# Two operand buffers lent to the first HGRN2 group, eviction priority, and a new order in cross-attention: a two-layer decoder trunk on one core

## The chip, the core and the metric

The kernel runs on one NeuronCore of a Trainium2 chip. Its engines are TensorE (PE; its weight loads are listed as PEld), VectorE (DVE), ScalarE (ACT), GpSimd (POOL) and SyncE (SP), which issues most DMAs. Each engine works through its own queue in order and waits at semaphores for the others. The metric is the device time of one execution in microseconds; the times given are medians over runs.

## What is computed

The reference is a trunk of two layers over 256 tokens of width 2048, followed by an RMSNorm. Layer 0 mixes tokens with eight HGRN2 heads (a gated linear recurrence) and eight gated-DeltaNet heads (delta rule); layer 1 with a Mamba-2 SSD mixer. After each mixer come a cross-attention of four heads into 256 memory tokens and a SwiGLU network. Cut to what matters here:

```
def hgrn2_gdn_mixer(u, ...):
    proj = u @ w_in
    a_q, a_f, a_i, a_g, b_q, b_k, b_v, b_g, b_beta, b_a = split(proj)
    o_a = hgrn2_chunked(silu(a_q), (1 - lb) * sigmoid(-a_f), a_i, log(lb + (1 - lb) * sigmoid(a_f)))
    o_a = gated_head_norm(o_a, hgrn_norm, a_g)       # times silu(a_g)
    o_b = gated_delta_chunked(...)                   # on silu(conv(b_q, b_k, b_v))
    o_b = gated_head_norm(o_b, gdn_norm, b_g)
    return concatenate([o_a, o_b]) @ w_out

def memory_cross_attention(h, m, wq, wk, wv, wo):
    q, k, v = heads(h @ wq), heads(m @ wk), heads(m @ wv)
    p = softmax(q k^T * 128 ** -0.5)
    return (p v) @ wo
```

## The kernel before

**Matmuls in three products.** Weights and activations are float32. Both are split into a high part in TensorE's float32r format and a low rest, and a product is summed from high x high, high x low and low x high. `xstat` (L183) does a projection of all 256 tokens onto up to 512 columns: two accumulators in PSUM (two token halves, from the pool `pa`, four buffers) and, for 16 tiles of 128 rows, 2 x 3 matmuls: 96 of 128x512. `wtiles` (L160) feeds it: a DMA of 512 KB into `wr`, a cast by ScalarE into `wh` (L157), a subtraction by VectorE into `wl` (L125), with four buffers of each. One such tile holds two of the 16 row blocks and feeds 12 matmuls.

**Leaving the accumulators.** `rows` copies the two accumulators through ScalarE, scaled by the norm's factor `r`, into the tile "raw" (one buffer). Where the function is a sigmoid, VectorE multiplies once more by the scaled input, which makes SiLU. `columns` then turns "raw" by TensorE transposes into the PSUM tile `tn`. `gate_rows` does the same without turning, into a tile of its own: "gate" or "vt" in the hybrid mixer, "XT" in attention. Each of these tags has one buffer: the next user waits until the last reader of the one before is done.

**The order.** The program is traced in Python order; a planner then orders the queue of every engine by simulating a timeline with its own durations. Of the instructions that it holds ready it takes the one that stands earliest in the program, and buffers are given out as they come free in that simulation. `later` pins some DMAs in program order.

**Layer 0's mixer** (`hybrid`) traces gdn(0), gdn(1), hgrn(0), hgrn(1) and then the output projection in two halves: `project(Wo, yb, 8, 8)` for the two gdn results and `project(Wo, ya, 0, 8)` for the two hgrn results, each in four blocks of 512 columns with 48 matmuls. Each of gdn and hgrn works on four heads. gdn ends in a serial chain: its matrix goes out to DRAM and comes back re-blocked, a 16x16 inversion runs on VectorE, the results X and XT go through DRAM again, then come three doubling levels of small matmuls (L578 to L599) and the outputs. hgrn forms its scores in seven levels, each a chain over VectorE, ScalarE, GpSimd and TensorE, into the tile "D", which gdn uses for its decays `E`. `finish` multiplies by the values, `head_norm` reads the gate, `head_out` writes the two operand tiles (high and low part) into the pool "u". That pool has 16 buffers of [128, 4, 256], which also hold the eight operand tiles of the layer's normed input.

**Cross-attention** (`xattn`) projects q from the tokens and k from the memory, takes the scores for two token halves `a`, two heads at a time in a PSUM tile of the pool `pm` (three buffers), and for each half in turn: maximum, exponential with its sum, reciprocal, four multiplications, then the transposes into `pT`:

```
        for a in range(2):
            ...
            for i in range(2):
            ...
                    act.activation(pr[:, a, m], ps[:, x], AF.Exp, bias=mx[:, m:m + 1], scale=sc,
                                   accum_out=sm[:, m:m + 1])
            dve.reciprocal(sm, sm)
            for m in range(4):
                dve.tensor_scalar(pr[:, a, m], pr[:, a, m], sm[:, m:m + 1], None, op0=ALU.mult)
            for b in range(2):
            ...
                dve.tensor_copy(pT[b][:, :, a * P:(a + 1) * P], ps)
        v = gate_rows(M, ("xa_wv", layer), 0, AF.Copy, "XT")
```

After that come the value products and the output projection `xa_wo` (four row tiles, so 24 matmuls for a block).

The functions that the diff touches, and what calls them:

Of the kernel before, what the change touches and what calls it, by code (L numbers as in the profile page):

```python
# [9 lines left out]
F32 = mybir.dt.float32  # L10
# [3 lines left out]
AF = mybir.ActivationFunctionType  # L14
ALU = mybir.AluOpType
AX = mybir.AxisListType
PSUM = bass.MemoryType.PSUM

P = 128
D = 2048  # L20
T = 256
# [57 lines left out]
def trunk(ctx: ExitStack, tc: tile.TileContext, A: dict, out: bass.AP):  # L79
# [44 lines left out]
    def tt(e, o, a, b, op):  # L124
        e.tensor_tensor(o, a, b, op=op)  # L125

    def stt(o, a, s, b, op0, op1):
        dve.scalar_tensor_tensor(o, a, s, b, op0=op0, op1=op1)  # L128

    def t4(tag, shape, dt=F32):  # L130
        return mp.tile(shape, dt, name=tag, tag=tag, bufs=BUFS.get(tag, 1))
# [219 lines left out]
    def conv(c, x, w):  # L351

        act.activation(c, x, AF.Copy, scale=w[:, 3:4])  # L353
        for s in range(1, 4):
            stt(c[:, s:T], x[:, 0:T - s], w[:, 3 - s:4 - s], c[:, s:T], ALU.mult, ALU.add)

    def rows(N, W, n0, func=AF.Copy, first=None):

        accs = xstat(W, n0, 512, N.u)
        if first:  # L360
            first()
        r = N.column()
        o = t4("raw", [P, 2, 512])
        o = [o[:, 0], o[:, 1]]
        for a in range(2):
            act.activation(o[a], accs[a], func, scale=r[:, a:a + 1])  # L366
            if func == AF.Sigmoid:
                stt(o[a], accs[a], r[:, a:a + 1], o[a], ALU.mult, ALU.mult)
        return o

    def columns(N, W, n0, func=AF.Copy, first=None):
# [63 lines left out]
    def head_out(yT, norm, g):  # L435
# [5 lines left out]
            stt(lo[:, m, :], ps, w, hi[:, m, :].bitcast(F32), ALU.mult, ALU.subtract)  # L441
        return hi, lo

    def gate_rows(N, W, n0, func=AF.Silu, tag="gate", n=512):
        o = t4(tag, [P, 2, 512])
        for c in range(0, 512, n):
            accs = xstat(W, n0 + c, n, N.u)
            r = N.column()
            for a in range(2):
                act.activation(o[:, a, c:c + n], accs[a], func, scale=r[:, a:a + 1])  # L450
                if func == AF.Sigmoid:
                    stt(o[:, a, c:c + n], accs[a], r[:, a:a + 1], o[:, a, c:c + n], ALU.mult, ALU.mult)
        return o


    def hybrid(N, nxt):
        W = ("hy_w_in", 0)
# [168 lines left out]
        def hgrn(g):  # L626
            kq = t4("kq", [P, 2, 4, T])
            lf = t4("tmp", [P, 4, T])
            for i, ps in columns(N, W, 1024 + 512 * g):
                act.activation(lf[:, 2 * i:2 * i + 2], ps, AF.Sigmoid)  # L630
                act.activation(kq[:, 0, 2 * i:2 * i + 2], ps, AF.Sigmoid, scale=-1.0)
            for m in range(4):
                dve.tensor_scalar(kq[:, 0, m], kq[:, 0, m], lb[:, 1, 4 * g + m:4 * g + m + 1], None, op0=ALU.mult)
            for i, ps in columns(N, W, 512 * g, AF.Sigmoid):
                act.copy(kq[:, 1, 2 * i:2 * i + 2], ps)
            gate = gate_rows(N, W, 3072 + 512 * g, AF.Sigmoid)
            G = t4("cv", [P, 4, T])
            for m in range(4):
                l0, l1 = lb[:, 0, 4 * g + m:4 * g + m + 1], lb[:, 1, 4 * g + m:4 * g + m + 1]
                act.activation(lf[:, m], lf[:, m], AF.Ln, bias=l0, scale=l1)  # L640
                for a in range(2):
                    sl = slice(a * P, (a + 1) * P)
                    dve.tensor_tensor_scan(G[:, m, sl], lv[:, len(LEVELS), :], lf[:, m, sl], 0.0,
                                           op0=ALU.mult, op1=ALU.add)
            k, q = kq[:, 0], kq[:, 1]
            S = t4("D", [P, 12, P])
            for i in range(2):
                ps = psb([P, 4, P])
                for x in range(4):
                    m, a = i * 2 + x // 2, x % 2  # L650
                    sl = slice(a * P, (a + 1) * P)
                    mm(ps[:, x], k[:, m, sl], q[:, m, sl])
                tt(dve, S[:, 4 * i:4 * i + 4], ps, ident.unsqueeze(1).to_broadcast([P, 4, P]), ALU.mult)
            for li, s in enumerate(LEVELS):
                nb = 1024 // (2 * s)
                vw = lambda t: t.rearrange("p h (b two s) -> p (h b) two s", two=2, s=s)
                Xl = t4("tmp", [P, 4, T])
                Xv, Gv = vw(Xl), vw(G)
                ref = Gv[:, :, 0, s - 1:s].to_broadcast([P, nb, s])
                tt(dve, Xv[:, :, 0, :], ref, Gv[:, :, 0, :], ALU.subtract)  # L660
                if s < 64:
                    tt(dve, Xv[:, :, 1, :], Gv[:, :, 1, :], ref, ALU.subtract)
                    act.activation(Xl, Xl, AF.Exp)  # L663
                else:
                    act.activation(Xv[:, :, 0, :], Xv[:, :, 0, :], AF.Exp)
                    act.activation(Xv[:, :, 1, :], Gv[:, :, 1, :], AF.Exp)
                tt(pool, Xv[:, :, 0, :], Xv[:, :, 0, :], vw(k)[:, :, 0, :], ALU.mult)
                tt(pool, Xv[:, :, 1, :], Xv[:, :, 1, :], vw(q)[:, :, 1, :], ALU.mult)
                ps = psb([P, 8, 64])
                for x in range(8):  # L670
                    m, a = x // 2, x % 2
                    xa = Xl[:, m, a * P:(a + 1) * P]
                    mm(ps[:, x].rearrange("p (b s) -> p b s", s=s), xa,
                       xa.rearrange("p (b two s) -> p b two s", two=2, s=s)[:, :, 1, :])
                right = lambda t: t.rearrange("p x (b two s) -> p x b two s", two=2, s=s)[:, :, :, 1, :]
                msk = right(lv[:, li, :].unsqueeze(1))
                dve.copy_predicated(right(S[:, 0:8]), msk.to_broadcast([P, 8, 64 // s, s]).bitcast(U32),
                                    ps.rearrange("p x (b s) -> p x b s", s=s))

            Xl = t4("tmp", [P, 4, T])  # L680
            G4 = G.rearrange("p h (a two s) -> p h a two s", a=2, two=2)
            tt(dve, G4[:, :, :, 1, :], G4[:, :, :, 1, :], G4[:, :, :, 0, 63:64].to_broadcast([P, 4, 2, 64]), ALU.add)
            tt(dve, Xl[:, :, 0:P], G[:, :, P - 1:P].to_broadcast([P, 4, P]), G[:, :, 0:P], ALU.subtract)
            act.activation(Xl[:, :, 0:P], Xl[:, :, 0:P], AF.Exp)
            act.activation(Xl[:, :, P:T], G[:, :, P:T], AF.Exp)
            tt(pool, Xl[:, :, 0:P], Xl[:, :, 0:P], k[:, :, 0:P], ALU.mult)
            tt(pool, Xl[:, :, P:T], Xl[:, :, P:T], q[:, :, P:T], ALU.mult)
            ps = psb([P, 4, P])
            for m in range(4):
                mm(ps[:, m], Xl[:, m, 0:P], Xl[:, m, P:T])  # L690
            act.copy(S[:, 8:12], ps)
            v = gate_rows(N, W, 2048 + 512 * g, AF.Copy, "vt").rearrange("p a (m d) -> p a m d", m=4)
            return finish(g, v, gate, lambda m: S[:, 2 * m], lambda m: S[:, 8 + m], lambda m: S[:, 2 * m + 1],
                          "hgrn_norm", EPS)

        yb = [gdn(0), gdn(1)]


        lg = col("lb", 0, 16)
# [19 lines left out]
    def xattn(layer, N, nxt):  # L719
# [15 lines left out]
        pT = [t4(tg, [P, 4, T]) for tg in ("D", "MD")]  # L735
        pr = t4("kq", [P, 2, 4, T])
        sc = float(P) ** -0.5
        for a in range(2):
            mx = cp.tile([P, 4], F32, name="xmx", tag="xmx", bufs=1)
            sm = cp.tile([P, 4], F32, name="xsm", tag="xsm", bufs=2)  # L740
            for i in range(2):
                ps = psb([P, 2, T])
                for x in range(2):
                    m = 2 * i + x
                    mm(ps[:, x], q[:, m, a * P:(a + 1) * P], k[:, m])
                dve.tensor_reduce(mx[:, 2 * i:2 * i + 2], ps, axis=AX.X, op=ALU.max)
                dve.tensor_scalar(mx[:, 2 * i:2 * i + 2], mx[:, 2 * i:2 * i + 2], -sc, None, op0=ALU.mult)
                for x in range(2):
                    m = 2 * i + x
                    act.activation(pr[:, a, m], ps[:, x], AF.Exp, bias=mx[:, m:m + 1], scale=sc,  # L750
                                   accum_out=sm[:, m:m + 1])
            dve.reciprocal(sm, sm)
            for m in range(4):
                dve.tensor_scalar(pr[:, a, m], pr[:, a, m], sm[:, m:m + 1], None, op0=ALU.mult)
            for b in range(2):
                ps = psb([P, 4, P])
                for m in range(4):
                    pe.transpose(ps[:, m], pr[:, a, m, b * P:(b + 1) * P], ident)  # L758
                dve.tensor_copy(pT[b][:, :, a * P:(a + 1) * P], ps)
        v = gate_rows(M, ("xa_wv", layer), 0, AF.Copy, "XT")  # L760
        hi, lo = utiles()
        for i in range(2):
# [254 lines left out]
```

## Time and profile before

| | |
|---|---|
| Median of 3 runs | 3005.39 us (3005.18 to 3006.37) |
| Profiled execution | 3001.37 us, its span 2999.6 us |
| TensorE busy | 2951.6 us, 98% |
| VectorE, ScalarE, GpSimd busy | 58%, 50%, 9% |
| Mean granted clock of TensorE | 0.992 |

The profile is of one execution. Times in its rows are microseconds from the start of the span unless marked ns. A row names the line, the engine, the operation, and output<-input by the program's tile names; a count follows an x. In square brackets, or behind "idle before", stands how long the engine had waited and for what. Since a helper issues all matmuls (L122) and most VectorE operations (L125, L128), those rows are told apart by their tiles. Matmuls overlap in the pipeline, so the spacing of their starts, not their mean duration, is what one costs in a row of them.

### The profile page before, as it was taken

How to read it: one execution, taken by the hardware profiler on the slowest of the kernel's cores; microseconds unless marked ns; L12 is line 12 of the kernel's file. 1: busy time of each engine (PE TensorE's matmuls, PEld its weight loads, DVE VectorE, ACT ScalarE, POOL GpSimd, SP SyncE). 2: the span in 40 equal slices, each digit the busy share in tenths (PEclk: the TensorE clock that was granted, in tenths of full speed). 3: DMA queues.
4: the chain of work that ended last, by engine and by line, in shares of the span. 5: the costliest groups of instructions: out<-in, count | busy, mean ns of one | idle time of the engine just before them, and what ended most of it. 6: DMA issues, size and time to landing. Idle time of an engine off the chain costs nothing.

```text
span 2999.6 us, 36568 instructions
## 1 busy us (share of the span) xinstructions
PE 2951.6 (98%) x13948; PEld 2448.5 (82%) x13948; DVE 1739.2 (58%) x2154; ACT 1513.3 (50%) x1933; POOL 265.2 (9%) x209
## 2 busy tenths in 40 slices
PE   9999799999999999999999999999999999999998
PEld 7888688878888888888888788878878888888887
DVE  6665577665555445445666646666655554445455
ACT  7445364565443444344567645766555444443444
POOL 1011233020000000000022300231000000000000
PEclk9999999999999999999999999999999999999999
DMA  7555334664666666666554466455656666666664
GB/s 280 171 168 156 100 116 144 184 203 150 189 189 196 189 191 189 195 191 184 182 162 155 158 187 189 150 158 164 189 176 188 189 188 193 191 189 192 193 190 148
DMA packets 152160, 533.35 MB, mean 178 GB/s; under 512 B 16592, under 2 KB 22864, under 8 KB 151984
## 3 DMA queue, kind: packets, MB, share of 16 engines
q1 hardware_dynamic: 150096, 526.15, 56.8%
q0 software_dynamic: 1472, 4.59, 0.5%
q8 instruction: 109, 1.79, 0.3%
q14 instruction: 67, 0.55, 0.1%
q10 hardware_dynamic: 416, 0.27, 0.0%
HBM read 526.49 MB, written 4.46 MB: 177 GB/s over the span
## 4 chain that ended last, share of the span: by engine, by line
PE 93%; issue 2%; DVE 1%; DMA 1%; POOL 1%; ACT 1%; SPq 0%; DVEq 0%; ACTq 0%; POOLq 0%
PE acc L122 86%; PE mx L122 5%; PE mx L280 1%; PE tn L280 1%; POOL tmp L125 1%; DVE wl L125 0%; DMA wr<-in_memT 0%; DVE b L125 0%; PE mx L853 0%; DMA XT<-scratch 0%; DMA b<-scratch 0%; DMA scratch<-b 0%; DMA wr<-in_hy_w_in 0%; PE mx L758 0%; DVE tmp L125 0%
## 5 line engine op out<-in xcount | busy, mean ns | idle before, releaser
L122 PE MATMUL acc<-wh,u 128*128 128x512 f32 (+1 forms) x7904 | 2455.1, 390 | 6.7 <-ACT wh L157 6.7
L125 DVE TENSOR_TENSOR wl<-wr,wh 128x1024 fp32r<-128x1024 f32 x980 | 1236.2, 1265 | 1052.5 <-ACT wh L157 1049.5
L122 PEld LDWEIGHTS acc<-wh,u 128*128 128x128 f32 x7904 | 1475.4, 188 | 305.9 <-ACT wh L157 6.7
L157 ACT CAST wh<-wr 128x1024 fp32r<-128x1024 f32 x980 | 1028.6, 1052 | 1149.4 <-PE acc L122 1076.4
L122 PE MATMUL acc<-wl,u 128*128 128x512 f32 (+1 forms) x3952 | 1538.5, 389 | 3.5 <-DVE wl L125 3.4
L122 PEld LDWEIGHTS acc<-wl,u 128*128 128x128 f32 x3952 | 744.0, 188 | 153.9 <-DVE wl L125 5.0
L125 POOL TENSOR_TENSOR tmp<-gh,cst 128x512 fp32r<-128x512 f32 x36 | 49.6, 1379 | 1303.2 <-ACT gh L157 849.3
L128 DVE SCALAR_TENSOR_TENSOR cv<-tn,cols,cv 128x255 f32<-128x255 f32 (+2 forms) x120 | 57.7, 481 | 31.3 <-ACT cv L353 28.6
L125 POOL TENSOR_TENSOR tmp<-tmp,kq 128x512 f32<-128x512 f32 x32 | 61.7, 1957 | 106.9 <-ACT tmp L663 95.9
L125 DVE TENSOR_TENSOR h<-h,acc 128x512 f32<-128x512 f32 (+1 forms) x84 | 52.3, 656 | 9.6 <-PE acc L122 9.4
L366 ACT ACTIVATE raw<-acc,r 128x512 f32<-128x512 f32 x66 | 43.5, 684 | 10.7 <-PE acc L122 10.6
L128 DVE SCALAR_TENSOR_TENSOR u<-mx,cols,u 128x256 fp32r<-128x256 f32 x96 | 42.9, 478 | 7.1 <-ACT u L301 6.7
L301 ACT ACTIVATE u<-mx,cols 128x256 fp32r<-128x256 f32 x80 | 34.7, 470 | 22.8 <-PE mx L280 18.8
L280 PE MATMUL tn<-cst,raw 128*128 128x128 f32 x272 | 45.5, 275 | 0.0
L280 PEld LDWEIGHTS tn<-cst,raw 128*128 128x128 f32 x272 | 35.0, 142 | 9.5
L125 DVE TENSOR_TENSOR u<-mx,u 128x512 fp32r<-128x512 f32 x48 | 31.0, 684 | 17.3 <-ACT u L157 17.3
L125 POOL TENSOR_TENSOR tmp<-gl,cst 128x512 fp32r<-128x512 f32 x36 | 40.3, 1120 | 0.1
L157 ACT CAST u<-mx 128x512 fp32r<-128x512 f32 x48 | 26.0, 592 | 27.7 <-PE mx L122 17.0
L122 PE MATMUL mx<-tmp,mr 128*128 128x512 f32 x108 | 36.2, 418 | 0.0
L125 POOL TENSOR_TENSOR MD<-MD,b 128x1536 f32<-128x1536 f32 x8 | 34.9, 4364 | 1.3 <-ACT MD L407 1.3
L122 PEld LDWEIGHTS mx<-tmp 128*128 128x128 f32 x240 | 29.3, 198 | 2.8 <-POOL tmp L125 2.2
L122 PE MATMUL mx<-tmp 128*128 128x64 f32 (+1 forms) x240 | 29.5, 281 | 2.0 <-POOL tmp L125 2.0
(260 smaller groups left out, 1312.3 us busy)
## 6 DMA issues: line engine op xcount, KB each, us to landing
wr<-in_ffn_w_gate SPq DMA_DIRECT2D x176, 512.0 KB, 3.7
wr<-in_ffn_w_up SPq DMA_DIRECT2D x176, 512.0 KB, 3.6
wr<-in_ffn_w_down SPq DMA_DIRECT2D x176, 512.0 KB, 3.6
wr<-in_ssd_w_in SPq DMA_DIRECT2D x162, 512.0 KB, 3.7
wr<-in_hy_w_in SPq DMA_DIRECT2D x130, 512.0 KB, 3.9
wr<-in_ssd_w_out SPq DMA_DIRECT2D x64, 512.0 KB, 4.1
wr<-in_hy_w_out SPq DMA_DIRECT2D x32, 512.0 KB, 3.6
wr<-in_xa_wq SPq DMA_DIRECT2D x16, 512.0 KB, 3.7
```

Of the source, the lines that this page charges most:

```text
L122: pe.matmul(o, lhsT=lhsT, rhs=rhs, start=start, stop=stop, skip_group_check=True)
L125: e.tensor_tensor(o, a, b, op=op)
L128: dve.scalar_tensor_tensor(o, a, s, b, op0=op0, op1=op1)
L157: act.copy(hi, src)
L280: pe.transpose(ps[:, x, a * P:(a + 1) * P], src[a][:, c * P:(c + 1) * P], ident)
L301: act.activation(hi[:, c], ps[:, x], AF.Copy, scale=g)
L366: act.activation(o[a], accs[a], func, scale=r[:, a:a + 1])
```

## The change

`rows` and `gate_rows` share a new function `evict`, which issues the same instructions under the planner's `high_priority`. In the hybrid mixer two tiles of the pool "u" are claimed between gdn(0) and gdn(1), each by a memset of one column on GpSimd, and hgrn(0) puts its gate and its value there instead of in "gate" and "vt"; hgrn(1) still uses those two. In attention the scores, maxima and exponentials of both token halves come first; the reciprocals, the multiplication (now one instruction for four heads, with the factor broadcast) and the transposes follow in a second loop, and the copies of the second memory half go to ScalarE.

```
+    def evict(o, accs, r, func):
+
+        with tc.high_priority():
+            for a in range(2):
+                act.activation(o[a], accs[a], func, scale=r[:, a:a + 1])
+                if func == AF.Sigmoid:
+                    stt(o[a], accs[a], r[:, a:a + 1], o[a], ALU.mult, ALU.mult)
+
     def rows(N, W, n0, func=AF.Copy, first=None):
...
-        for a in range(2):
-            act.activation(o[a], accs[a], func, scale=r[:, a:a + 1])
-            if func == AF.Sigmoid:
-                stt(o[a], accs[a], r[:, a:a + 1], o[a], ALU.mult, ALU.mult)
+        evict(o, accs, r, func)
         return o
...
+    def operand_home():
+
+        o = up.tile([P, 2, 512], F32, name="uf", tag="u")
+        pool.memset(o[:, 0, 0:1], 0.0)
+        return o
+
     def gate_rows(N, W, n0, func=AF.Silu, tag="gate", n=512):
-        o = t4(tag, [P, 2, 512])
+        o = t4(tag, [P, 2, 512]) if isinstance(tag, str) else tag
         for c in range(0, 512, n):
             accs = xstat(W, n0 + c, n, N.u)
-            r = N.column()
...
+            evict([o[:, a, c:c + n] for a in range(2)], accs, N.column(), func)
         return o
...
-            gate = gate_rows(N, W, 3072 + 512 * g, AF.Sigmoid)
+            gate = gate_rows(N, W, 3072 + 512 * g, AF.Sigmoid, "gate" if g else homes[0])
...
-            v = gate_rows(N, W, 2048 + 512 * g, AF.Copy, "vt").rearrange("p a (m d) -> p a m d", m=4)
+            v = gate_rows(N, W, 2048 + 512 * g, AF.Copy, "vt" if g else homes[1]).rearrange("p a (m d) -> p a m d", m=4)
...
-        yb = [gdn(0), gdn(1)]
+        yb = [gdn(0)]
+        homes = [operand_home(), operand_home()]
+        yb.append(gdn(1))
...
+        sm = cp.tile([P, 2, 4], F32, name="xsm", tag="xsm")
+        mx = cp.tile([P, 2, 4], F32, name="xmx", tag="xmx")
         for a in range(2):
-            mx = cp.tile([P, 4], F32, name="xmx", tag="xmx", bufs=1)
-            sm = cp.tile([P, 4], F32, name="xsm", tag="xsm", bufs=2)
             for i in range(2):
...
-            dve.reciprocal(sm, sm)
-            for m in range(4):
-                dve.tensor_scalar(pr[:, a, m], pr[:, a, m], sm[:, m:m + 1], None, op0=ALU.mult)
+        for a in range(2):
+            dve.reciprocal(sm[:, a], sm[:, a])
+            tt(dve, pr[:, a], pr[:, a], sm[:, a].unsqueeze(2).to_broadcast([P, 4, T]), ALU.mult)
             for b in range(2):
                 ps = psb([P, 4, P])
                 for m in range(4):
                     pe.transpose(ps[:, m], pr[:, a, m, b * P:(b + 1) * P], ident)
-                dve.tensor_copy(pT[b][:, :, a * P:(a + 1) * P], ps)
+                (act.copy if b else dve.tensor_copy)(pT[b][:, :, a * P:(a + 1) * P], ps)
```

## Rows read from the trace of the kernel before

**Rows 1.** The page, busy time by engine.

```profile
PE 2951.6 (98%) x13948; PEld 2448.5 (82%) x13948; DVE 1739.2 (58%) x2154; ACT 1513.3 (50%) x1933; POOL 265.2 (9%) x209
```

**Rows 2.** The chain that ended last: start, duration, what.

```profile
890.12 147.39 PE acc L122 x650
```

**Rows 3.** Waits of TensorE, whole span: total, times, longest.

```profile
PE mx L122 <- DMA XT<-scratch: 9.2, 1, 9.2
PE mx L758 <- DVE kq L754: 8.0, 2, 4.6
```

**Rows 4.** Weight matmuls by stretch: length, busy (count), clock, DMA share, GB/s.

```profile
328.95:368.60 39.65, 0.00 (x0) 0.83 0.25 83
```

**Rows 5.** All of TensorE's matmuls in the same stretch.

```profile
328.95:368.60 39.65, 24.72 (x175) 0.83 0.25 83
```

**Rows 6.** ScalarE's timeline: start, duration, line, operation.

```profile
366.72 1.27 ACT L450 ACTIVATE vt<-acc,r 128x512 f32<-128x512 f32 x2
...
376.78 1.27 ACT L450 ACTIVATE gate<-acc,r 128x512 f32<-128x512 f32 x2
```

**Rows 7.** GpSimd's timeline, gdn(0).

```profile
141.30 0.12 POOL L564 MEMSET b<- 64x16 f32 x1
```

**Rows 8.** TensorE's timeline, the chains of gdn(0) and of gdn(1).

```profile
173.98 1.05 PE L122 MATMUL mx<-XT,b 128*128 128x128 f32 x8
...
188.00 1.06 PE L122 MATMUL mx<-b,X 128*128 128x128 f32 x8
188.90 1.06 PE L122 MATMUL mx<-XT,b 128*128 128x128 f32 x8
...
235.11 1.73 PE L122 MATMUL mx<-w,D 128*128 128x128 f32 x14
...
338.11 2.04 PE L122 MATMUL mx<-XT,b 128*128 128x128 f32 x8 [9.19 <-DMA XT<-scratch]
...
366.04 2.84 PE L122 MATMUL mx<-w,D 128*128 128x128 f32 x24
```

**Rows 9.** VectorE's timeline, hgrn(1)'s output and the output projection.

```profile
528.93 0.87 DVE L128 SCALAR_TENSOR_TENSOR u<-mx,cols,u 128x256 fp32r<-128x256 f32 x2
...
560.30 1.28 DVE L125 TENSOR_TENSOR h<-h,acc 128x512 f32<-128x512 f32 x2
```

**Rows 10.** ScalarE's timeline, hgrn(1)'s first level and its query.

```profile
445.04 1.06 ACT L663 ACTIVATE tmp<-tmp 128x1024 f32<-128x1024 f32 x1
...
452.98 0.59 ACT L635 COPY kq<-tn 128x512 f32<-128x512 f32 x1 [1.85 <-PE tn L280]
```

**Rows 11.** Groups of instructions by form: busy, mean ns, idle before.

```profile
L125 DVE TENSOR_TENSOR wl<-wr,wh 128x1024 fp32r<-128x1024 f32 x980 | 1236.2, 1265 | 1052.5 <-ACT wh L157 1049.5
L157 ACT CAST wh<-wr 128x1024 fp32r<-128x1024 f32 x980 | 1028.6, 1052 | 1149.4 <-PE acc L122 1076.4 <-issue 25.5 <-DMA wr<-in_hy_w_in 9.2
...
L366 ACT ACTIVATE raw<-acc,r 128x512 f32<-128x512 f32 x66 | 43.5, 684 | 10.7 <-PE acc L122 10.6
...
L848 ACT ACT_TABLE_LOAD x22 | 28.2, 1283 | 1.3
...
L754 DVE TENSOR_SCALAR kq<-kq,xsm 128x256 f32<-128x256 f32 x16 | 4.6, 348 | 0.2
```

**Rows 12.** TensorE's timeline, attention of layer 0.

```profile
654.72 1.03 PE L122 MATMUL mx<-X,cv 128*128 128x256 f32 x4
...
666.48 0.39 PE L122 MATMUL acc<-wh,u 128*128 128x512 f32 x1
...
680.74 0.59 PE L122 MATMUL mx<-D,XT 128*128 128x256 f32 x2
681.17 0.59 PE L122 MATMUL mx<-MD,XT 128*128 128x256 f32 x2
681.41 0.58 PE L122 MATMUL acc<-wh,u 128*128 128x512 f32 x1
```

**Rows 13.** Engines by stage: length, busy of PE, PEld, DVE, ACT, POOL, clock, DMA.

```profile
660.00:680.00 20.00, 15.21 (x64) 12.14 (x63) 11.23 (x24) 7.27 (x17) 0.00 (x0) 0.83 0.34 106
```

More of the change, by code (lines that the diff above doesn't have):

```diff
@@ L442, in head_out @@
         return hi, lo
+    def operand_home():
+        o = up.tile([P, 2, 512], F32, name="uf", tag="u")
+        pool.memset(o[:, 0, 0:1], 0.0)
+        return o
     def gate_rows(N, W, n0, func=AF.Silu, tag="gate", n=512):
-        o = t4(tag, [P, 2, 512])
+        o = t4(tag, [P, 2, 512]) if isinstance(tag, str) else tag
         for c in range(0, 512, n):
             accs = xstat(W, n0 + c, n, N.u)
-            r = N.column()
[L449 to L452, printed above, removed]
+            evict([o[:, a, c:c + n] for a in range(2)], accs, N.column(), func)
         return o
@@ L745, in xattn @@
                     mm(ps[:, x], q[:, m, a * P:(a + 1) * P], k[:, m])
-                dve.tensor_reduce(mx[:, 2 * i:2 * i + 2], ps, axis=AX.X, op=ALU.max)
-                dve.tensor_scalar(mx[:, 2 * i:2 * i + 2], mx[:, 2 * i:2 * i + 2], -sc, None, op0=ALU.mult)
+                mi = mx[:, a, 2 * i:2 * i + 2]
+                dve.tensor_reduce(mi, ps, axis=AX.X, op=ALU.max)
+                dve.tensor_scalar(mi, mi, -sc, None, op0=ALU.mult)
                 for x in range(2):
                     m = 2 * i + x
-                    act.activation(pr[:, a, m], ps[:, x], AF.Exp, bias=mx[:, m:m + 1], scale=sc,
-                                   accum_out=sm[:, m:m + 1])
-            dve.reciprocal(sm, sm)
-            for m in range(4):
-                dve.tensor_scalar(pr[:, a, m], pr[:, a, m], sm[:, m:m + 1], None, op0=ALU.mult)
+                    act.activation(pr[:, a, m], ps[:, x], AF.Exp, bias=mx[:, a, m:m + 1], scale=sc,
+                                   accum_out=sm[:, a, m:m + 1])
+        for a in range(2):
+            dve.reciprocal(sm[:, a], sm[:, a])
+            tt(dve, pr[:, a], pr[:, a], sm[:, a].unsqueeze(2).to_broadcast([P, 4, T]), ALU.mult)
             for b in range(2):
```

## The prediction

> **What bounds the kernel now.** I read the page first: TensorE is busy for 98% of the span, no other engine for more than 58% [rows 1]. The chain that ended last says the same: outside a few stretches it is one run of weight matmuls, 650 of them in 147.39 us [rows 2], so 0.2268 us for each 128x512 product. No edit here touches those products, and where they run back to back nothing can be won. What is left is the time in which TensorE waits or runs slow.
>
> So the second view was TensorE's waits: the two largest named ones inside the kernel are 9.2 us for the DMA of XT, in gdn(1), and 8.0 us in two pieces for the scaled probabilities, one piece in each attention [rows 3]. The third view was the time by stage. Between 328.95 and 368.60 not one weight matmul ran [rows 4], though TensorE counts as busy for 24.72 us: 175 small matmuls of gdn(1)'s own chain, at a mean granted clock of 0.83 [rows 5].
>
> Why it had nothing else to do stands in ScalarE's timeline. The accumulators of hgrn(0)'s value are copied out at 366.72 and those of its gate at 376.78 [rows 6]. These are two pairs, and the pool holds two pairs; both were complete when the last weight matmul ended before 328.95. Their homes, "vt" and "gate", were still gdn(1)'s. TensorE starved for want of a place to put two finished results.
>
> **Hybrid stage, first part of the change.** The homes come from the pool "u", which has 16 buffers: eight for the operand blocks, two for gdn(0)'s output, two for the homes, two for gdn(1), two for hgrn(0). That is 16, and hgrn(1)'s pair needs the homes only after hgrn(0) has read them; before, the same place was its own. So the homes cost no wait that I can see. The two claims are one-column memsets on GpSimd; the nearest row, a 64x16 memset, took 0.12 us [rows 7], so 0.24 us on an engine that is busy for 9%. The evictions gain a wait on them, satisfied some 80 us before; behind them in ScalarE's queue stand weight casts.
>
> With both pairs free at about 329, hgrn(1)'s forget and query projections can run under gdn(1)'s chain: 2 x 96 x 0.2268 = 43.5 us, more than the 39.65 us that are open. What the small matmuls need at full clock is read from gdn(0), which ran the same chain with weights between: eight take 188.90 - 188.00 = 0.90 us, 0.112 each [rows 8]. So 175 x 0.112 = 19.6 us of the 39.65 are work, and **20.1 us** are loss. That is the ceiling of this part.
>
> It isn't the forecast. The weights that are moved forward are then missing as cover, and the chain itself gets longer: gdn(0)'s, with weights between, took from 173.98 to 236.84, 62.9 us, gdn(1)'s, bare, from 338.11 to 368.88, 30.8 us [rows 8]. hgrn(0) can't write its scores before gdn(1) gives up tile "D" at the end of that chain. So hgrn(0), hgrn(1), and with them the second output operand can be late by up to 62.9 - 30.8 = 32.1 us. How much lateness is free? That operand is complete at 529.8, and the first output block that needs it was added at 560.30 [rows 9], so its 48 matmuls (10.9 us) began near 549.4: 19.6 us of slack, which the 20.1 us brought forward just use up. What helps: hgrn(1)'s first level was exponentiated at 446.10 and then waited for the query, in place at 453.57 [rows 10], which its early projection makes up to 7.5 us earlier; the first half of an output block needs only hgrn(0) (5.4 us); and where cover runs out, the chain goes at its bare pace. The bounds: if the chain stretches by all of 32.1 us and only the half block helps, 20.1 - 32.1 + 5.4 = -6.6 us, a loss; if it doesn't stretch, +20.1 us. I take half the stretch, 16 us, less the 7.5 us and half of the 5.4 us: about 6 us lost, **14 us gained**.
>
> **Evictions at high priority.** No instruction is added. An eviction of two 128x512 halves takes 2 x 0.684 = 1.4 us and goes ahead of a cast; a cast takes 1.05 us, and ScalarE idles 1076.4 us in all before 980 casts for TensorE to free a buffer, 1.1 us each [rows 11]. A weight tile feeds 12 matmuls, 2.7 us, and there are four of them in the ring. So I cost it at nothing; the cover is that ring. If it didn't cover, each of the 33 evictions into "raw" (66 halves [rows 11]) could cost up to 1.4 us, and more where a table load (1.28 us [rows 11]) comes with it.
>
> **Attention.** In layer 0 the last matmul of xa_wv starts at 666.48 and ends near 666.87, and the first of xa_wo starts at 681.41 [rows 12]: 14.5 us, in a stage with a clock of 0.83 [rows 13]. Into it fall 16 transposes at the 0.112 us above, and 8 score and 16 value matmuls of 256 columns, 0.215 us each (680.74 to 681.17 for two [rows 12]): 1.8 + 5.2 = 7.0 us of work, 7.5 us of loss. Layer 1 waits 4.6 us for the probabilities where layer 0 waits 3.4 (8.0 in all [rows 3]), so about 8.7 us there: a ceiling of 16.2 us.
>
> The loss has one cause: the second token half's score tiles are put behind the transposes of the first half, and its softmax then runs when xa_wv is used up. With all four score tiles issued first, they go under xa_wv. VectorE and ScalarE have from the first score tile, at 654.72 [rows 12], to 667 for it. In its place remain, after xa_wv, the eviction of the value (1.4 us) and the copy of the last transposed probabilities before the value products, and one cast before xa_wo: near 2 us a layer. Gain 16.2 - 4 = **12 us**. Bounds: 2 us, if the fourth score tile, for which the three buffers of pool "pm" leave no room until the first is exponentiated, drags the softmax past xa_wv again; 16.2 us.
>
> The multiplication changes too: four tensor_scalar of 348 ns, each for 256 elements, become one tensor_tensor of 1024 with a broadcast factor. The nearest row for it is the weights' subtraction, also 1024 elements, at 1265 ns [rows 11]; the four took some 1.1 us end to end, overlapped. So 0.1 to 0.2 us more, twice a layer, under xa_wv: nothing. The Trainium skill ("VectorE: DVE Perf Modes", section "The perf-mode tier table") speaks against this edit: on fp32 in SBUF a tensor_scalar streams at twice the rate of a tensor_tensor. By that rule alone the multiplication would take up to twice as long, by an estimate some 1 us more each time and 4 us in all if none of it were hidden; the rows show that the starts of four instructions eat most of that advantage. The copies of the second memory half move to ScalarE, which idles there; I count nothing.
>
> **Sum.** The profiled execution took 3001.37 us around a span of 2999.6 us; the three runs have a median of 3005.39. 14 + 12 = 26 us: the profiled execution would come to 2975, the median to **2979 us**. A measurement of this kernel can tell about 0.2%, 6 us, from no change.
>
> **Rivals.**
> (a) *Both parts pay in full*: 20 + 16 us, 2969 us or below. For it: gdn(0) shows that the planner fills such a chain. Against: the stretch above. Chance 0.13.
> (b) *The hybrid's gain comes back as a wait*: cover spent early, hgrn(1) late, TensorE idle ahead of the output product; only attention pays: 3005.4 - 12 = 2993 us, 2988 to 2998. For it: the 62.9 us of gdn(0). Against: the slack and the 7.5 us. Chance 0.20.
> (c) *The change doesn't do what it says*: the planner, which works with durations of its own, puts the homes' evictions or the fourth score tile where they were. Then the waits of [rows 3] stay: 3000 to 3008, about 3004 us. Chance 0.08.
> (d) *Slower*: the evictions push the casts, ScalarE switches tables between sigmoid and exponential for them, and the ring runs dry. The SSD stage has 20 of the 33; each, with two extra loads, takes 1.4 + 2.6 = 4 us of ScalarE. It decides from the point where a cast comes later than the ring's 4 x 2.7 us of work ahead of TensorE; at 2 us of TensorE for each of 20 it costs 40 us, 26 of them paid by the gains: 3005.4 - 26 + 40 = 3019 us. Against: half of ScalarE is idle. Chance 0.07.
> The forecast, 2970 to 2988, has 0.52.
>
> **Range and chances.** From the full gain to case (b): 2965 to 2998 us; of the cases it leaves out nearly all of (c) and (d). Faster by over 0.2%: the forecast, (a) and most of (b), 0.84. Within 0.2%: most of (c) and a little of (b), 0.09. Slower: (d), 0.07.
>
> **What would show it.** Right: the gate and value of hgrn(0) leave their accumulators near 330, weight matmuls run between 329 and 369, and the wait for XT is gone; gdn(1)'s chain lengthens toward 60 us. In attention the waits for kq are gone, and xa_wo starts about 8 us after xa_wv ends. Wrong: a new wait of TensorE on hgrn(1)'s operands between 500 and 570; a wait on wh in the SSD stage, which has none now; the group period of that stage longer. The weak term is the stretch of gdn(1)'s chain: the whole difference between (a) and (b) hangs on it.

## The result

The change made the kernel faster: **2978.35 us** median of 4 runs (2977.38 to 2979.66), against 3005.85 us of the kernel before beside it (3005.18 to 3006.37), a ratio of 0.9909 with a 95% interval of 0.9892 to 0.9926. That is 27.5 us less; the forecast was 2979 us, 26 us less. A later pair of the same kernels gave 2979.07 and 3004.07 us, 0.9919 (0.9904 to 0.9934). The traces differ by less, 2999.6 against 2977.9 us of span, mostly because the profiled execution of before was 4 us shorter than that kernel's median.

### The profile page after: what moved, and what is told of

Read it like the earlier page. It is cut to its first block, busy times and chain, and to the rows that moved or that the text cites. A ratio compares the mean times of both kernels' runs of the same rounds, so it can differ in the third digit from the quotient of the medians.

```text
span 2977.9 us, 36564 instructions
## 1 busy us (share of the span) xinstructions
PE 2943.9 (99%) x13948; PEld 2443.6 (82%) x13948; DVE 1736.4 (58%) x2138; ACT 1517.2 (51%) x1939; POOL 258.8 (9%) x211
## 4 chain that ended last, share of the span: by engine, by line
PE 95%; DVE 1%; DMA 1%; ACT 1%; issue 1%; POOL 1%; SPq 0%; DVEq 0%; ACTq 0%; POOLq 0%
PE acc L122 87%; PE mx L122 5%; PE mx L280 1%; PE tn L280 1%; DMA wr<-in_memT 0%; POOL tmp L125 0%; PE mx L863 0%; DMA XT<-scratch 0%; DVE wl L125 0%; DMA scratch<-b 0%; ACT wh L157 0%; PE mx L438 0%; DVE tmp L125 0%; ACT u L254 0%; DMA wr<-in_hy_w_in 0%
## 5 line engine op out<-in xcount | busy, mean ns | idle before, releaser
L308 ACT ACTIVATE b<-h 128x512 f32<-128x512 f32 x48 | 29.9, 624 | 2.2 <-DVE h L128 2.0
```

The costliest lines, as they stand in the source:

```text
L308: act.activation(t4("b2", [P, 512]), src[:, a], AF.Square, accum_out=self.ss[:, a, nb:nb + 1])
```

## The profile after

The page first. The engines do what they did [rows 1], and TensorE is busy for 7.7 us less, which fits small matmuls that ran at a low clock and now run at full clock:

```profile
PE 2943.9 (99%) x13948; PEld 2443.6 (82%) x13948; DVE 1736.4 (58%) x2138; ACT 1517.2 (51%) x1939; POOL 258.8 (9%) x211
```

TensorE's waits in the kernel after (total, times, longest), to be held against [rows 3]: the wait for the probabilities fell from 8.0 to 0.3 us, that for XT only from 9.2 to 5.4, and one on "b" is new. "b" is the normed output of an hgrn group: 4.1 us are for that of hgrn(1), the other 1.8 us for that of hgrn(0).

```profile
PE mx L438 <- DVE b L128: 5.9, 2, 4.1
PE mx L122 <- DMA XT<-scratch: 5.4, 1, 5.4
...
PE mx L768 <- DVE kq L125: 0.3, 1, 0.3
```

ScalarE's timeline after. The gate and the value of hgrn(0) leave their accumulators at 305 to 330, where they left at 376.78 and 366.72 [rows 6]:

```profile
305.35 0.69 ACT L361 ACTIVATE uf<-acc,r 128x512 f32<-128x512 f32 x1
...
328.70 1.37 ACT L361 ACTIVATE uf<-acc,r 128x512 f32<-128x512 f32 x2 [0.17 <-PE acc L122]
```

So weight matmuls run where none ran [rows 4]. The weight matmuls after, in that stretch and in a later one (length, busy and count of TensorE, of its loads, VectorE, ScalarE, then clock, DMA share, GB/s):

```profile
328.95:368.60 39.65, 25.27 (x99) 19.62 (x98) 0.00 (x0) 1.48 (x3) 0.91 0.54 178
...
527.00:561.00 34.00, 18.97 (x74) 14.14 (x73) 0.07 (x1) 0.00 (x0) 0.90 0.30 93
```

The second row is the price. All matmuls of that later stretch, in the same view, with GpSimd's busy time as a fifth engine: TensorE is busy for 29.31 of 34.00 us, so it stands for 4.7 us, 4.1 of them in one hole, and the mean granted clock is 0.90.

```profile
527.00:561.00 34.00, 29.31 (x162) 24.98 (x161) 21.70 (x38) 11.14 (x16) 9.59 (x6) 0.90 0.30 93
```

TensorE's timeline after: gdn(1)'s chain, the hole, and the attention of layer 0.

```profile
340.62 2.05 PE L122 MATMUL mx<-XT,b 128*128 128x128 f32 x8 [5.38 <-DMA XT<-scratch]
...
358.93 1.06 PE L122 MATMUL mx<-XT,b 128*128 128x128 f32 x8
...
366.61 1.06 PE L122 MATMUL mx<-XT,b 128*128 128x128 f32 x8
...
405.59 1.73 PE L122 MATMUL mx<-w,D 128*128 128x128 f32 x14
...
543.85 1.95 PE L122 MATMUL mx<-vt,D 128*128 128x128 f32 x16
...
549.89 2.29 PE L438 MATMUL mx<-cst,b 128*128 128x128 f32 x8 [4.10 <-DVE b L128]
552.32 0.80 PE L122 MATMUL acc<-wh,u 128*128 128x512 f32 x1
...
661.81 0.40 PE L122 MATMUL acc<-wh,u 128*128 128x512 f32 x1
662.04 1.04 PE L768 MATMUL mx<-cst,kq 128*128 128x128 f32 x8
663.36 1.17 PE L768 MATMUL mx<-cst,kq 128*128 128x128 f32 x8 [0.28 <-DVE kq L125]
665.87 0.67 PE L122 MATMUL mx<-D,XT 128*128 128x256 f32 x2 [1.34 <-DVE D L769]
...
669.21 0.58 PE L122 MATMUL acc<-wh,u 128*128 128x512 f32 x1
```

Two readings. gdn(1)'s chain, which took 30.8 us bare [rows 8], now takes from 340.62 to 407.3, 66.7 us: its steps are 366.61 - 358.93 = 7.68 us apart, and 22 weight matmuls (22 x 0.2268 = 5.0 us) stand between two of them. In attention the gap from xa_wv's last matmul to xa_wo's first is 669.21 - 662.2 = 7.0 us, before 14.5 [rows 12].

VectorE's timeline after, with hgrn(1)'s operand "u" and blocks of the output projection "h" [rows 9], and one multiplication of the attention:

```profile
525.80 1.27 DVE L125 TENSOR_TENSOR h<-h,acc 128x512 f32<-128x512 f32 x2
...
552.30 1.94 DVE L128 SCALAR_TENSOR_TENSOR u<-mx,cols,u 128x256 fp32r<-128x256 f32 x4 [0.74 <-ACT u L445]
...
588.97 1.28 DVE L125 TENSOR_TENSOR h<-h,acc 128x512 f32<-128x512 f32 x2
...
656.65 1.23 DVE L125 TENSOR_TENSOR kq<-kq,xsm 128x1024 f32<-128x1024 f32 x1
```

hgrn(1)'s operand is complete at 554.2, where it was 529.8: 24.4 us late. **The theory** to test: the hybrid mixer's gain is its ceiling of 20.1 us less what is still waited for XT (5.4) and less the hole (4.7), 10 us, and the hole comes from the chain that was stretched by weights. (This sum leaves out the low clock behind both waits; what they cost when they are taken away stands below.) **Rivals**: the priority of the evictions makes or eats the gain; the cover is short, whatever the chain does; tile "D" holds hgrn(0) back; one part eats what another wins.

## The parts one by one

Each kernel was timed beside the kernel before, and the ratio is to those runs; that kernel had medians of 3003.7 to 3005.9 us. The first four stand beside 3005.31.

**homes_only**: the two operand buffers, evictions at their usual priority.

```
-    gate = gate_rows(N, W, 3072 + 512 * g, AF.Sigmoid)
+    gate = gate_rows(N, W, 3072 + 512 * g, AF.Sigmoid, "gate" if g else homes[0])
...
+    homes = [operand_home(), operand_home()]
```

> The two borrowed buffers alone: evictions in their ordinary place in the order, attention as before. Theory A (the places were what TensorE lacked): the borrowed buffers carry the hybrid stage's gain by themselves, weight matmuls run through the stretch that was empty (329 to 369), and the kernel gains what the two profiles show up to the feed-forward stage less attention's share: 12.2 - 5.7 = 6.5 us, so 4 to 9 us. Theory B (the eviction priority does it, a home without it is filled too late): under 2 us.

Measured: 2998.57 us, ratio 0.9979 (0.997 to 0.9988), 6.7 us less than 3005.31.

**prio_only**: `evict` under high priority, no homes.

```
+        with tc.high_priority():
             for a in range(2):
                 act.activation(o[a], accs[a], func, scale=r[:, a:a + 1])
```

> Eviction priority alone: homes and attention as before. Theory A: within 2 us of the kernel before, since TensorE never waits for an eviction outside the two stages; at most the 0.9 us that the SSD stage shows between the two profiles. Theory B: 4 us or more gained. A third way, that ahead of the casts they delay the weights: slower by some us, with waits of TensorE on the cast.

Measured: 3005.79 us, 1.0001 (0.9992 to 1.001). Alone, the priority neither wins nor costs.

**homes_prio**: both, the whole hybrid part.

> Both hybrid edits together, attention as before. If the parts add: the sum of the two single runs, some 7 us gained by the profiles. If priority and homes need each other: clearly more than the sum. The changed kernel less this one is attention's share: 14 us by the profiles (5.7 in layer 0, 8.5 in layer 1), 12 by the prediction.

Measured: 2995.12 us, 0.9967 (0.9955 to 0.998), 10.2 us less. With the homes the priority adds 3.4 us by the medians. The intervals of the two ratios overlap, but the runs themselves do not: the slowest of homes_prio took 2995.79 us, the fastest of homes_only 2996.89. Where the 3.4 us arise was not tried; the longest wait on "b" is 4.8 us in homes_only and 4.1 in homes_prio, and the value leaves at 330.24 and at 329.12.

**attn_only**: the kernel before with the attention edit alone.

> The attention edit alone, the hybrid mixer and the evictions as before. If attention stands for itself: 14 us gained, 5.7 in layer 0 and 8.5 in layer 1, and the waits for the scaled probabilities gone from both. If it needs the value's eviction to go first: a new wait of TensorE for the value behind the last projection matmul, and under 10 us.

Measured: 2989.48 us, 0.995 (0.9937 to 0.9964), 15.8 us less. 10.2 + 15.8 = 26.0 us of the 27.5: within what medians here move the parts add, and neither eats the other.

**order_only**: of the attention edit only the order; four tensor_scalar and the copies on VectorE stay.

```
-            dve.reciprocal(sm, sm)
-            for m in range(4):
-                dve.tensor_scalar(pr[:, a, m], pr[:, a, m], sm[:, m:m + 1], None, op0=ALU.mult)
+        for a in range(2):
+            dve.reciprocal(sm[:, a], sm[:, a])
+            for m in range(4):
+                dve.tensor_scalar(pr[:, a, m], pr[:, a, m], sm[:, a, m:m + 1], None, op0=ALU.mult)
```

> The kernel before, with only the order of the attention changed: all four score tiles first, then the four multiplications (kept as tensor_scalar) and the transposes of either token half, both copies kept on VectorE. If the order alone carries the attention part, the time is that of the attention edit as a whole, 2989.5 within 1.5 us. If the single multiplication and the copies moved to ScalarE carry a share, the time is 2991 to 2997.

Measured: 2986.6 us (before 3005.07), 0.9942 (0.9929 to 0.9956), the attention part's gain in full. The four multiplications in VectorE's timeline of this kernel, beside the single one of 1.23 us above:

```profile
668.54 1.15 DVE L756 TENSOR_SCALAR kq<-kq,xsm 128x256 f32<-128x256 f32 x4
```

Four took 1.15 us and one takes 1.23 us. By the Trainium skill ("VectorE: DVE Perf Modes", section "The perf-mode tier table") a tensor_scalar streams fp32 at twice the rate of a tensor_tensor. In these two rows the sign agrees, but with instructions this short the difference is 0.08 us and not a factor of two.

## What holds the hybrid's gain back

**one_home_gate**: a home for the gate alone; the value waits for "vt".

```
-    v = gate_rows(N, W, 2048 + 512 * g, AF.Copy, "vt" if g else homes[1])
+    v = gate_rows(N, W, 2048 + 512 * g, AF.Copy, "vt")
```

> The kernel after, with a home for the gate of hgrn(0) alone; its value waits for tile vt as before. One pair of accumulators is free from 310 us on, the other is held until gdn(1) gives up vt near 390 to 400. If one free pair feeds TensorE as well as two, the time is 2978.4 within 2 us. If TensorE needs both (one filling while the other is copied out), it starves between two projections and the time is 2982 to 2988.

Measured: 2977.46 us (2976.30 to 2983.77) beside 2979.07 for the kernel after: no difference that the runs can tell. ScalarE's timeline of this run shows the value held until "vt" is free, and the weights ran all the same, 209 weight matmuls from 340 to 410 against 204:

```profile
397.51 1.26 ACT L361 ACTIVATE vt<-acc,r 128x512 f32<-128x512 f32 x2 [2.33 <-PE mx L122]
```

One free pair of accumulators feeds TensorE through the chain.

The same trace says something about the theory too. gdn(1)'s chain is as long as after, from 339.83 to 405.2, and yet the hole between 527 and 561 is gone: TensorE is busy for 33.32 of the 34.00 us, at full clock. It stands earlier instead, for 5.2 us between 460 and 500, where the kernel after stands for 1.8. The last matmuls of this run's chain, then all engines by stretch (columns as above):

```profile
403.47 1.73 PE L122 MATMUL mx<-w,D 128*128 128x128 f32 x14
```

```profile
460.00:500.00 40.00, 34.85 (x199) 28.80 (x198) 34.77 (x60) 26.01 (x35) 7.69 (x4) 1.00 0.36 112
...
527.00:561.00 34.00, 33.32 (x173) 27.61 (x172) 24.16 (x42) 15.36 (x23) 3.60 (x2) 1.00 0.42 126
```

So a chain of that length need not end in that hole. Where TensorE stands hangs also on which weights are still left to run by then; that was not tried by itself.

**scores_md**: hgrn(0)'s scores go to a tile "MD" instead of "D".

```
-            S = t4("D", [P, 12, P])
+            S = t4("D" if g else "MD", [P, 12, P])
```

> The kernel after, with hgrn(0)'s scores in a tile of tag MD instead of D, so that they wait for gdn(1)'s last reader of MD (about 394 us) and not of D (407 us). If the late release of D at the end of the lengthened chain is what makes hgrn(1) late, its second operand is complete some 10 us earlier than 554, the hole at 540 to 560 closes, and the time falls by 4 to 8 us from 2978.4, to 2970 to 2974. If hgrn(1) is late for another reason (its query and its own level chain are queued behind weights), the operand stays near 554 and the time within 2 us of 2978.4.

Measured: 2980.41 us, 1.3 us above 2979.07 and 2.1 above 2978.35: no gain. TensorE's timeline of this run: "MD" is given up near 395.9, but hgrn(0)'s first scores (mx<-kq) stay behind the last transposes of gdn(1), as they did after (418.51):

```profile
394.80 1.05 PE L122 MATMUL mx<-w,MD 128*128 128x128 f32 x8
...
418.87 0.81 PE L438 MATMUL mx<-cst,b 128*128 128x128 f32 x6
419.52 1.06 PE L122 MATMUL mx<-kq 128*128 128x128 f32 x8
```

So the tile alone isn't what chains hgrn(0) to gdn(1). What does (the planner's order, or the PSUM pool "pm") was not tried.

**xt_first**: XT written and read back ahead of X.

```
-            for q, (d, t) in enumerate(((d_x, X), (d_t, XT))):
+            for q, d, t in ((1, d_t, XT), (0, d_x, X)):
```

> The kernel after, with the transposed operand XT of a gdn group written to its scratch and read back ahead of X. The XT transfer is issued about 2.2 us earlier. If the 5.4 us wait of TensorE for XT is the price of transfer latency on the path, the wait falls to about 3 us, gdn(1)'s chain starts 2 us earlier and the time falls by 2 to 4 us, to 2974 to 2976. If the wait is covered again downstream (the hole behind the output product is set by something else) or X becomes the late one, the time stays within 1.5 us of 2978.4.

Measured: 2980.03 us, and the wait 4.9 us. The run tells nothing of the theory: in its trace GpSimd issues X at 333.01 and XT at 334.77, the old order, so the transfer didn't move.

**keys_early**: the memory's key projection (96 weight matmuls) between the halves of the output projection, as cover for the hole.

```
         project(Wo, yb, 8, 8)
+        keys.append(mem_keys(0))
         project(Wo, ya, 0, 8, lambda nb: nxt.block(nb, h[nb]))
```

> The kernel after, with the memory key projection of the first cross-attention (96 weight matmuls, 21.8 us at 0.2268 us each) traced between the two halves of the hybrid's output projection. If the missing gain is cover that was used up (weights moved under gdn(1)'s chain, none left while hgrn(1) finishes), these matmuls fill the hole at 527 to 561 and the wait on b, and the time falls by 5 to 8 us, to 2970 to 2973. If cover is not the cause, or the key projection was itself cover in the attention stage, the time stays within 2 us of 2978.4 or rises.

Measured: 2988.34 us (0.9949, 0.9936 to 0.9961), 9 to 10 us slower than the kernel after. Weight matmuls of this run in the stretch of the hole, and ScalarE's timeline:

```profile
527.00:561.00 34.00, 10.16 (x33) 8.16 (x34) 0.00 (x0) 0.00 (x0) 0.70 0.19 57
```

```profile
525.75 1.04 ACT L157 CAST wh<-wr 128x1024 fp32r<-128x1024 f32 x1 [3.71 <-DMA wr<-in_xa_wk]
...
550.29 1.70 ACT L254 ACTIVATE u<-wr,cols 128x256 fp32r<-128x256 f32 x4
```

33 weight matmuls instead of 74, at a clock of 0.70. The memory's own operand tiles were built only from 550.29 on, behind hgrn(1)'s output in ScalarE's queue, while its first weights (in_xa_wk) had been cast at 525.75, ahead of the hgrn half of the output projection. It was work, but not work that was ready.

**paced**: the direct test. Thirty weight matmuls of hgrn(1)'s forget projection stay free, the other 66 are issued behind given steps of gdn(1)'s chain, and the later projections behind its last step. `chain` is the list of the last matmul of each step; no work and no wait on another engine is added.

```
+        if W[0] != "hy_w_in" or not chain or n0 not in PACED or first and k < FREE:
+            return nullcontext()
+        return tc.issue_after(chain[min(3 * (k - FREE) // 2, len(chain) - 1) if first else -1])
...
+            with behind(W, n0, k):
                 for a in range(2):
```

> The kernel after, with hgrn(1)'s projections kept from crowding gdn(1)'s chain on TensorE: 30 weight matmuls of the forget projection run free while XT is on its way, the other 66 are each issued behind a given step of the chain, and the query, gate and value projections behind its last step. If hgrn(1) is late because 22 weight matmuls (5.0 us) stand between two steps that need about 1 us of cover, the chain takes 175 x 0.112 + 80 x 0.2268 = 38 us and ends near 380 instead of 407, hgrn(1)'s second operand is complete some 20 us earlier than 554, the hole at 540 to 555 with its low clock is gone, and the time falls by 5 to 9 us to 2970 to 2974. If the steps need more cover than that, or the gain was lost elsewhere, TensorE idles within the chain instead and the time stays within 2 us of 2978.4 or rises.

Measured: **2972.12 us** (0.9895, 0.9879 to 0.9912), beside 2979.07 for the kernel after: 7.0 us less. TensorE's timeline of this run (its lines stand 2 or more higher), VectorE's, and the weight matmuls by stretch:

```profile
339.99 2.05 PE L124 MATMUL mx<-XT,b 128*128 128x128 f32 x8 [5.43 <-DMA XT<-scratch]
...
352.37 1.05 PE L124 MATMUL mx<-XT,b 128*128 128x128 f32 x8
...
356.90 1.06 PE L124 MATMUL mx<-XT,b 128*128 128x128 f32 x8
...
379.46 1.73 PE L124 MATMUL mx<-w,D 128*128 128x128 f32 x14
```

```profile
534.12 0.87 DVE L130 SCALAR_TENSOR_TENSOR u<-mx,cols,u 128x256 fp32r<-128x256 f32 x2
...
536.49 0.48 DVE L130 SCALAR_TENSOR_TENSOR u<-mx,cols,u 128x256 fp32r<-128x256 f32 x1
...
581.35 1.28 DVE L127 TENSOR_TENSOR h<-h,acc 128x512 f32<-128x512 f32 x2
```

```profile
328.00:340.00 12.00, 6.57 (x29) 5.10 (x28) 0.00 (x0) 1.37 (x2) 0.92 0.96 311
...
527.00:561.00 34.00, 33.18 (x144) 26.41 (x143) 3.91 (x6) 0.00 (x0) 1.00 0.61 185
```

The steps are 4.5 us apart here, and 5.0 on either side, with 8 to 10 weight matmuls in each, where after they are 7.68 us apart with 22; the chain is over at 381.2 instead of 407.3; hgrn(1)'s operand is complete at 537.0 instead of 554.2; 144 weight matmuls run at full clock where the hole was. The wait for XT (first row) is as in the kernel after.

**paced_xt**: in addition, the first matmul that reads XT is issued behind the ninth of the forget projection's sixteen row blocks. The pace changes with it: the other seven, and the query projection after them, follow the steps one row block at a time.

```
+            if W[0] == "hy_w_in" and n0 == PACED[0] and k == FREE - 1:
+                for x in xt_first:
+                    tc.add_manual_dep(x, i.name, mybir.DependencyInfo(
+                        mybir.DependencyClass.NoSync, mybir.DependencyReason.DATA), reason="cover")
```

> The kernel of the run before (projections paced behind gdn(1)'s chain), with the first matmul that reads XT issued behind the ninth of the sixteen pairs of weight rows of the forget projection (28 weight matmuls, 6.4 us, more ahead of it), and the rest of the forget and the query projection paced behind the steps. If the 5.4 us wait for XT is only a wrong place in TensorE's order, it vanishes and the time falls by 4 to 6 us, from 2972.1 to 2966 to 2968. If the weights that would fill it are not there in time (their transfer or cast is late), the wait is named after wh or wl instead and the time stays within 2 us of 2972.

Measured: **2967.26 us** (0.9879, 0.9863 to 0.9896; before beside it 3003.74), 4.9 us less than paced. Its wait for XT, its weight matmuls in the stretch where paced has 29, and VectorE's addition of the last block of the output projection:

```profile
PE mx L124 <- DMA XT<-scratch: 0.6, 1, 0.6
```

```profile
328.00:340.00 12.00, 12.00 (x55) 9.93 (x54) 0.00 (x0) 1.37 (x2) 1.00 0.94 301
```

```profile
576.45 1.28 DVE L127 TENSOR_TENSOR h<-h,acc 128x512 f32<-128x512 f32 x2
```

What it keeps are waits of 2.1 us on "b" and 1.7 us on GpSimd's "tmp", where paced has 0.2 and 0.7.

**after_again**: the kernel after on the chip of paced and one_home_gate.

> The kernel after, unchanged, on the chip of the two runs beside it: 2978.4 within 2 us.

Measured: 2979.07 us (2978.0 to 2980.98).

## Why the prediction held, step by step

**What bounds.** Right that TensorE starved for want of free accumulators; too strong that both results needed a place. One place does as much (one_home_gate).

**The hybrid's ceiling, 20.1 us.** Right, and it can be had. paced and paced_xt add 7.0 and 4.9 us to the 10.2, together 22.1 us by the medians. By the traces the last of the eight blocks of the output projection is added at 595.76 in the kernel before and at 576.45 in paced_xt (above), 19.3 us earlier.

**The hybrid's forecast, 14 us.** Measured 10.2: terms of it were mis-sized. The wait for XT was counted as gone and kept 5.4 of its 9.2 us; taking it away was worth 4.9 us (paced_xt). The loss at the output projection, forecast at 6 us, was 7.0 (what paced won back). That is nearly right, but the terms behind it weren't:

- "I take half the stretch, 16 us" failed: the chain grew by 66.7 - 30.8 = 36 us, more than even the bound of 32.1, because the planner put 22 weight matmuls between two steps that need a fifth of that as cover. Bare, in the kernel before, the same steps were 3.68 us apart with 24 matmuls of 0.112 (2.7 us) in each: 1.0 us to cover, 4 to 5 weight matmuls.
- As cover the prediction counted half of the 5.4 us of one half block, 2.7 us. Between the last gdn block (525.80) and the hole TensorE ran 46 weight matmuls, 10.4 us.

Bare steps in TensorE's timeline of before; weight matmuls after, from the last gdn block to the hole (TensorE alone, clock, DMA share, GB/s):

```profile
346.57 1.16 PE L122 MATMUL mx<-X,b 128*128 128x128 f32 x8 [0.72 <-ACT b L589]
...
350.25 1.16 PE L122 MATMUL mx<-X,b 128*128 128x128 f32 x8 [0.73 <-ACT b L589]
```

```profile
525.80:545.80 20.00, 11.48 (x46) 1.00 0.47 144
```

The pacing removed the hole and won 7.0 us, and the later place of XT's reader removed that wait and won 4.9 us. That the longer chain makes the hole by itself isn't shown: one_home_gate has a chain as long and no hole there. What the query's early projection (7.5 us in the prediction) is worth was not measured by itself.

The sum does not close to the microsecond. 20.1 - 7.0 - 4.9 = 8.2, against 10.2 by the medians and 6.8 by the traces: the last block is added at 588.97 after and at 595.76 before. attn_only, whose hybrid code is that of before, adds it at 600.01, 4.3 us later, with a wait of 2.1 us on "b" that the trace of before lacks. A difference of 2 us lies below that. The theory's 20.1 - 5.4 - 4.7 = 10.0 meets 10.2 by luck, since it leaves out the low clock behind the two waits.

VectorE's timeline of before, then of attn_only, last block:

```profile
595.76 1.28 DVE L125 TENSOR_TENSOR h<-h,acc 128x512 f32<-128x512 f32 x2
```

```profile
600.01 1.28 DVE L125 TENSOR_TENSOR h<-h,acc 128x512 f32<-128x512 f32 x2
```

**"hgrn(0) can't write its scores before gdn(1) gives up tile D."** The order is as said, the reason isn't: with another tile nothing moved (scores_md).

**The priority, nothing.** Right alone (prio_only), and the waits named no ring that ran dry in the SSD stage; rival (d) is out. Beside the homes it is worth 3.4 us, which the prediction did not have; the reason stays open.

**Attention, 12 us.** The mechanism was right and the size low: 15.8 us, with an interval from 10.8 to 18.9 that holds 12 and the ceiling of 16.2. The mis-sized term is the 2 us reckoned to remain in each layer: in layer 0 0.28 + 1.34 = 1.6 us of waits are left, in layer 1 one wait of 0.3 us. Order alone carries it (order_only). The fourth score tile did not drag: in layer 0 the last score matmuls start at 655.91, and xa_wv runs until 661.81.

**Rivals.** (b) came half true: the hole stands where it was placed, between 500 and 570, at a third of its price, 7.0 of the 20.1 us. (a) is what paced_xt reaches, with two more edits. (c) is out. That the forecast came within 2 us of the gain is in part luck: one term was too high by 4 us and the other too low by 4.

## What to carry to other kernels

Weights laid under a serial chain of small matmuls are cover to be rationed: count what one step needs (here 1.0 us, 4 to 5 of the big matmuls) and stay near it, since every further one delays the chain and is missing later, when the chain's result is waited for. Here 8 to 10 in a step instead of 22 won 7.0 us; fewer were not tried. Work offered as cover must have its own operands ready and its weights in the right place of the ring, or it widens the hole. Where a softmax stands between two projections, issue every score tile before the first turn of probabilities.

## What the runs showed of the hardware that was not expected

After the idle 4.10 us at 549.89 the eight transposes took 2.29 us, where the eight of the attention took 1.04, and the first weight matmuls started 0.43 us apart instead of 0.2268. The granted clock was 0.50 there, the lower of the two levels (1.2 against 2.4 GHz), until about 555; from 555 to 557 it was 1.00. All matmuls of the kernel after (TensorE alone, clock, DMA share, GB/s):

```profile
549.89:552.20 2.31, 2.17 (x8) 0.50 0.00 0
```

In keys_early, where TensorE stood still for longer, the granted clock of the stretch from 527 to 561 was 0.70 against 0.90. A hole costs its length and then again a part of what follows: 4.7 us of standing still here, and 7.0 us won when it went.

Ahead of XT lies a gap that is not what the view of the chain makes of it. For the kernel after the chain of waits shows 8.74 us of "issue" before GpSimd's transfer at 327.20, time in which nothing is waited for. VectorE's timeline tells what happened:

```profile
318.46 8.74 issue x2
```

```profile
322.56 1.21 DVE L125 TENSOR_TENSOR wl<-wr,wh 128x1024 fp32r<-128x1024 f32 x1
323.70 1.33 DVE L125 TENSOR_TENSOR b<-b,b 64x55 f32<-64x55 f32 x6
324.95 1.21 DVE L125 TENSOR_TENSOR wl<-wr,wh 128x1024 fp32r<-128x1024 f32 x1
326.09 0.60 DVE L125 TENSOR_TENSOR b<-b,b 64x28 f32<-64x28 f32 x3
326.72 0.38 DVE L578 COPY b<-b 64x256 f32<-64x256 f32 x1
```

VectorE is still inverting: the last steps of the inversion and the transposed copy of its result end at 327.10, 0.1 us before the transfer. Between those steps stand subtractions for weight tiles of 1.21 us each, two of them in these rows. What the XT chain would gain if they stood behind the inversion was not tried.
